# Delta stage: keys of a chunk transposed once and scaled for both scan directions, with the second direction's scaled keys kept in DRAM until its visit

## Chip, cores and metric

The kernel runs on one core of a Trainium2 chip. The metric is the device time of one execution in microseconds (us). The engines are TensorE (PE, whose weight loads are listed as PEld), VectorE (DVE), ScalarE (ACT), GpSimd (POOL) and SyncE (SP), which issues most of the transfers. [...]

## What is computed

The program is one layer of a hybrid backbone over 128 context tokens and 2048 latent tokens. The part that matters here is a gated delta rule, run once forward and once backward over the tokens, with four heads of 128 by 128 state each:

```python
def gated_delta_chunked(q, k, v, g, beta, s0):
    """S_t = a_t (I - b_t k_t k_t^T) S_{t-1} + b_t k_t v_t^T, o_t = S_t^T q_t."""
    ...
    def step(s, inp):
        q_i, k_i, u_i, w_i, g_i, qk_i = inp
        v_new = u_i - jnp.einsum("bhck,bhkv->bhcv", w_i, s)
        o_i = (jnp.einsum("bhck,bhkv->bhcv", q_i * jnp.exp(g_i)[..., None], s)
               + jnp.einsum("bhcs,bhsv->bhcv", qk_i, v_new))
        g_last = g_i[..., -1:]
        s = (s * jnp.exp(g_last)[..., None]
             + jnp.einsum("bhck,bhcv->bhkv", k_i * jnp.exp(g_last - g_i)[..., None], v_new))
        return s, o_i
    ...
o_fwd, s_fwd = gated_delta_chunked(q, k, v, g[:, :, 0], beta[:, :, 0], s_init[:, 0])
o_bwd, s_bwd = gated_delta_chunked(q[:, ::-1], k[:, ::-1], v[:, ::-1], ...)
o = o_fwd + o_bwd[:, ::-1]
```

The state update needs the keys of a chunk, scaled by `exp(g_last - g_i)`, with tokens on partitions. That scale differs between the directions; the keys do not.

## The kernel before

The delta stage takes about 785 to 1095 us of the span. It handles the context chunk `CTX` and 16 latent chunks of 128 tokens in 17 iterations t = 0 to 16. Iteration 0 visits `CTX` in both directions, and iteration t visits chunk t-1 in the forward direction (d = 0) and chunk 16-t in the backward direction (d = 1). So each latent chunk is visited twice: for the first time in t = 1 to 8 and for the second time in t = 9 to 16. The last visit of a direction updates no state.

One visit is the generator `chain(d, c)`. It loads the values `tv`, transposes the keys `kt` on PE into the PSUM tile `pkt` (L906, four 128 by 128 transposes) and scales them by `kd` into `ks` on ACT (L909, four instructions). After that come `p1` from the state `S` (L917), `rh` on DVE (L923), `p2` (L927) and `on` (L934), `p3` from X and rh (L938), its copy `y` on ACT (L940), `p5` from ks and y (L945) and the new state `Sn` on DVE (L951), and `p4` (L957) with its sum on DVE (L961). The state is the chain from one iteration to the next. The first two steps of a visit in iteration t+1 (values, transposes, scaling) are written in iteration t by `start_chain`.

Work that a visit needs is prepared ahead. `prepare` (two iterations ahead) loads keys and a decay row `d_g`, builds `dm` on DVE (L819) and ACT (L820), makes `na` (L832), the product `pq` on PE (L840) for a chunk's first visit, and `pt` on DVE (L846). `combine` (one iteration ahead) loads the inverted 32 by 32 blocks `xc` from the DRAM tensor `d_x` (L853), spreads them on POOL into `X` (L855) and completes the 128 by 128 inverse with small matmuls (L868, L874, L877, L888, L892) and ACT copies. The blocks are inverted by `invert` on POOL for several chunks at once; the inversions started in t = 2, 4 and 8 (called inversion 2, 3 and 4 here) lie inside this stage. An inversion loads `W` from DRAM (L141, eight transfers), works on POOL, copies one part on ACT (`xo`, L159) and stores 16 pieces to `d_x` (L166).

The PSUM pool `pre` has two buffers, which `pkt` and `pq` share. `ks` has four SBUF buffers. The order of the instructions on each engine is fixed when the program is built, by a scheduler that follows its own estimate of times; every engine then runs its list in order, and a transfer that waits on SP holds back all later ones on SP.

Of the kernel before, what the change touches and what calls it, by code (L numbers as in the profile page):

```python
# [7 lines left out]
F32 = mybir.dt.float32  # L8
F32R = mybir.dt.float32r
BF16 = mybir.dt.bfloat16  # L10
AF = mybir.ActivationFunctionType
# [3 lines left out]
P = 128  # L15
# [4 lines left out]
NT = NTOK // P  # L20
CTX = NT - 1
H = 4
# [25 lines left out]
def hybrid_step_kernel(ctx, tc, x, wmod, pv, rows, win, wab, wout, wup, wdown, s0, cst,  # L48
                       y_prompt, y_sample, state, dbg=None):
    nc = tc.nc  # L50
# [4 lines left out]
    dr = ctx.enter_context(tc.tile_pool(name="dr", bufs=1, space=DRAM))  # L55

    d_kq = dr.tile([NT, P, 2, H, P], F32, name="d_kq")
    d_v = dr.tile([NT, P, H, P], F32, name="d_v")
    d_z = dr.tile([NT, P, H, P], F32, name="d_z")
    d_uc = dr.tile([NT, P, 4, P], F32, name="d_uc")  # L60
    d_mix = dr.tile([NT, P, 8, P], F32, name="d_mix")
# [46 lines left out]
    kd = cd.tile([P, 2, NT, H], F32, name="kd")  # L108
# [8 lines left out]
    def chunk(d, t):  # L117
        return CTX if t == 0 else t - 1 if d == 0 else 16 - t
# [647 lines left out]
            f(*args)  # L766


    RB = dict(kt=8, dm=7, ka=7, na=6, qt=5, pt=4, X=7, xc=2, ys=6, y2=2, tv=6, ks=4, rh=2, y=2, on=6)
    sW = ExitStack()  # L770
    with ExitStack() as s2:
        kap = s2.enter_context(tc.tile_pool(name="kap", bufs=2, reuse_waits="tile"))
# [6 lines left out]
        ck = s2.enter_context(tc.tile_pool(name="ck", bufs=2, reuse_waits="tile"))  # L779
# [18 lines left out]
        def fetch(key, make, src):  # L798
            if key in kept:
                return kept[key]  # L800
            t = make()
            nc.sync.dma_start(t[:], src)
            if key[0] in KEEP:
                kept[key] = t
            return t
# [4 lines left out]
        def prepare(d, c):  # L810
            kt = fetch((c, 0), lambda: kqp.tile([P, H, P], F32, name="kt", tag="kt", bufs=RB["kt"]), d_kq[c, :, 0])
            dm = kqp.tile([P, H, P], F32, name="dm", tag="dm", bufs=RB["dm"])
            t = [chunk(d, i) for i in range(NT)].index(c)
# [9 lines left out]
            else:  # L823
                ka, new = kap.tile([P, 2, 512], F32, name="ka", tag="ka", bufs=RB["ka"]), c not in raw
                if new:
# [3 lines left out]
                else:  # L829
                    nc.sync.dma_start(ka[:], d_a[:, :, c])  # L830
            na = kqb.tile([P, H, P], F32, name="na", tag="na", bufs=RB["na"])
            nc.vector.tensor_tensor(f(na[:]), ka[:, 0], f(dm[:]), ALU.mult)  # L832
            res = [na, None, kt, None]
            yield res
            qt = fetch((c, 1), lambda: pk.tile([P, H, P], F32, name="qt", tag="qt", bufs=RB["qt"]), d_kq[c, :, 1])
            pq = ka[:, 1]
            if new:
# [4 lines left out]
                if c not in KEEP:  # L842
                    pq = pqt[:]
                    nc.sync.dma_start(d_a[:, 1, c], ka[:, 1])
            pt = pk.tile([P, H, P], F32, name="pt", tag="pt", bufs=RB["pt"])
            nc.vector.tensor_tensor(f(pt[:]), pq, f(dm[:]), ALU.mult)  # L846
# [48 lines left out]

        st = {}

        def chain(d, c):
            kq = prep[d, c]
            tv = fetch((c, 2), lambda: kqc.tile([P, H, P], F32, name="tv", tag="tv", bufs=RB["tv"]), d_v[c])  # L900
            yield
            final = c == chunk(d, NT - 1)
            if not final:
                pk_ = pre.tile([P, H, P], F32, name="pkt", tag="pre")
                for h in range(H):
                    nc.tensor.transpose(pk_[:, h], kq[2][:, h], ident[:])  # L906
                ks = ck.tile([P, H, P], F32, name="ks", tag="ks", bufs=RB["ks"])
                for h in range(H):
                    nc.scalar.activation(ks[:, h], pk_[:, h], AF.Copy, scale=kd[:, d, c, h:h + 1])  # L909
            yield  # L910
            S = st[d]
            X = mats[d, c]
            pt = prep[d, c][1]
# [5 lines left out]
            rh = tv  # L919
            if S is not None:  # L920
                rh = ck.tile([P, H, P], F32, name="rh", tag="rh", bufs=RB["rh"])
# [7 lines left out]
            on = (fp if first else lp).tile([P, H, P], F32, name="on", tag="on", bufs=16 if first else RB["on"])  # L929
# [9 lines left out]
            y = ck.tile([P, H, P], F32, name="y", tag="y", bufs=RB["y"])  # L939
# [58 lines left out]
        def start_chain(t):  # L998
            if t > 16:
                return []  # L1000
            gens = [chain(d, c) for d, c in items(t)]
            for g in gens:
                next(g)
                next(g)
            return gens
# [210 lines left out]
    if True:  # L1216
# [187 lines left out]
        c = order3[-1]  # L1404
# [216 lines left out]
```

## Time and profile before

| | |
|---|---|
| Time, median of 3 runs | 2793.93 us (2784.18 to 2797.48) |
| Profiled execution | 2791.89 us; its span 2790.1 us |
| Mean granted clock of TensorE | 0.972 |
| PE busy, whole span | 2654.8 us (95%) |
| DVE, ACT, POOL busy | 1907.2, 1153.1, 789.9 us (68%, 41%, 28%) |
| DMA moved | 526.79 MB, mean 189 GB/s |

The profile is of one execution. Its engine times are in us from the start of the span. A busy share over the whole span mixes stages; the delta stage is a ninth of it, and there DVE, ACT, POOL and SP take turns with PE in holding the next step back.

### The profile page before, as it was taken

The page shows a single profiled execution, that of the slowest core. Times are in us where ns is not written, and L with a number is a line of the kernel's source. Part 1 is how long each engine was busy: PE and PEld are TensorE (multiplying, and loading weights), DVE is VectorE, ACT ScalarE, POOL GpSimd, SP SyncE. Part 2 cuts the span into 40 slices and gives each one's busy share as a digit, 9 for nine tenths or more (in the row PEclk, how much of TensorE's full clock was granted, in tenths as well). Part 3 has the DMA queues.
Part 4 walks back from the last instruction along what each step waited for, and adds up shares of the span by engine and source line. Part 5 has one row for each costly group of instructions (what it writes and reads, how often), then busy time and mean ns, then how long its engine had stood idle before and what let it go on. Part 6 is the DMA issues. An engine that isn't in the chain of part 4 may idle for free.

```text
span 2790.1 us, 41624 instructions
## 1 busy us (share of the span) xinstructions
PE 2654.8 (95%) x15309; PEld 2237.8 (80%) x15309; DVE 1907.2 (68%) x2840; ACT 1153.1 (41%) x2421; POOL 789.9 (28%) x851
## 2 busy tenths in 40 slices
PE   7999999979888998999899999999999999999998
PEld 4888888767778887888788888888888878888887
DVE  3898999885657785444687777887888873225343
ACT  5423132355656666666544444432222232224221
POOL 2211011166335683222666666500000000000000
PEclk9999999989969999999999999999999999999999
DMA  7024531576597565665777777888777754236453
GB/s 275 20 72 119 151 109 43 104 190 134 154 279 195 141 227 207 219 231 184 256 278 266 265 271 262 279 263 255 235 232 222 230 184 134 94 104 211 165 173 119
DMA packets 426712, 526.79 MB, mean 189 GB/s; under 512 B 144790, under 2 KB 301964, under 8 KB 426252
## 3 DMA queue, kind: packets, MB, share of 16 engines
q1 hardware_dynamic: 406380, 506.30, 57.5%
q10 hardware_dynamic: 20128, 17.83, 1.9%
q8 instruction: 121, 1.98, 0.3%
q14 instruction: 83, 0.68, 0.1%
HBM read 342.13 MB, written 181.90 MB: 188 GB/s over the span
## 4 chain that ended last, share of the span: by engine, by line
PE 61%; DMA 5%; DVE 4%; ACT 3%; SPq 3%; POOL 2%; issue 2%; ACTq 0%; DVEq 0%; POOLq 0%
PE ps L1318 10%; PE ps L1320 10%; PE ps L1319 10%; PE ps L1147 7%; PE ps L1486 6%; PE ps L1484 6%; PE ps L1485 6%; PE psc L1232 2%; SPq L166 1%; DVE dm L819 1%; PE p L938 1%; PE p L945 1%; DMA dm<-d_g 1%; DMA d_mix<-bigB 1%; PE p L957 1%
## 5 line engine op out<-in xcount | busy, mean ns | idle before, releaser
L1377 DVE SCALAR_TENSOR_TENSOR pa<-gb,pvf,pa 128x512 f32<-128x512 f32 (+1 forms) x704 | 491.0, 733 | 65.3 <-ACT pa L1375 62.5
L1318 PE MATMUL ps<-T,wr 128*128 128x512 f32 x1232 | 480.5, 391 | 0.1
L1319 PE MATMUL ps<-T,wr 128*128 128x512 f32 x1232 | 479.9, 389 | 0.0
L1320 PE MATMUL ps<-T,wr 128*128 128x512 f32 x1232 | 479.0, 390 | 0.6 <-POOL wr L1246 0.6
L361 PE MATMUL ps<-hH,wr 128*128 128x512 f32 (+1 forms) x960 | 349.7, 369 | 6.6 <-ACT bigA L412 3.8
L362 PE MATMUL ps<-hL,wr 128*128 128x512 f32 (+1 forms) x960 | 352.4, 367 | 0.0
L363 PE MATMUL ps<-hH,wr 128*128 128x512 f32 (+1 forms) x960 | 350.6, 366 | 0.0
L1484 PE MATMUL ps<-wd,yr 128*128 128x512 f32 x748 | 292.5, 391 | 6.1 <-ACT yr L1480 5.5
L1486 PE MATMUL ps<-wd,yr 128*128 128x512 f32 x748 | 292.1, 391 | 0.4 <-DVE yr L1481 0.4
L1485 PE MATMUL ps<-wd,yr 128*128 128x512 f32 x748 | 292.1, 391 | 0.0
L1318 PEld LDWEIGHTS ps<-T,wr 128*128 128x128 f32 x1232 | 231.4, 188 | 49.2 <-issue 0.8
L1320 PEld LDWEIGHTS ps<-T,wr 128*128 128x128 f32 x1232 | 231.4, 188 | 49.1 <-POOL wr L1246 1.1
L1319 PEld LDWEIGHTS ps<-T,wr 128*128 128x128 f32 x1232 | 231.4, 188 | 47.4
L375 DVE SCALAR_TENSOR_TENSOR acc<-bigA,pvt,acc 128x1024 f32<-128x1024 f32 (+2 forms) x168 | 252.3, 1502 | 13.2 <-ACT acc L372 9.2
L361 PEld LDWEIGHTS ps<-hH,wr 128*128 128x128 f32 x960 | 184.0, 193 | 33.5 <-ACT bigA L412 4.2
L1481 DVE TENSOR_TENSOR yr<-yt,yr 128x1408 fp32r<-128x1408 f32 x68 | 110.5, 1625 | 143.4 <-ACT yr L1480 143.3
L363 PEld LDWEIGHTS ps<-hH,wr 128*128 128x128 f32 x960 | 185.4, 193 | 25.4 <-issue 3.0
L362 PEld LDWEIGHTS ps<-hL,wr 128*128 128x128 f32 x960 | 185.3, 193 | 24.0 <-issue 1.6
L1351 POOL TENSOR_TENSOR up<-up,x 128x512 f32<-128x512 f32 x44 | 57.3, 1302 | 413.2 <-ACT pa L1383 217.9
L375 DVE SCALAR_TENSOR_TENSOR acc<-bigC,pvt,acc 128x1024 f32<-128x1024 f32 (+2 forms) x108 | 156.6, 1461 | 24.9 <-DMA bigB<-d_uc 15.5
L1484 PEld LDWEIGHTS ps<-wd,yr 128*128 128x128 f32 x748 | 141.0, 188 | 36.6 <-ACT yr L1480 6.5
L1486 PEld LDWEIGHTS ps<-wd,yr 128*128 128x128 f32 x748 | 141.0, 188 | 30.7 <-DVE yr L1481 1.4
(360 smaller groups left out, 4571.2 us busy)
## 6 DMA issues: line engine op xcount, KB each, us to landing
d_w<-wr SPq DMA_DIRECT2D x154, 512.0 KB
wr<-d_w SPq DMA_DIRECT2D x154, 512.0 KB
yt<-d_y SPq DMA_DIRECT2D x68, 704.0 KB
raw<-in_wup_dram SPq DMA_DIRECT2D x60, 512.0 KB
xt<-in_x_dram SPq DMA_DIRECT2D x34, 512.0 KB
wmt<-in_wmod_dram SPq DMA_DIRECT2D x24, 512.0 KB
wt<-in_win_dram SPq DMA_DIRECT2D x24, 512.0 KB
wmt<-in_wmod_dram SPq DMA_DIRECT2D x48, 256.0 KB
```

What stands on the lines that cost most here:

```text
L361: nc.tensor.matmul(ps[:, 0:n], wr[:, 0, k], hH[bi][:, k], start=(k == 0), stop=False)
L362: nc.tensor.matmul(ps[:, 0:n], wr[:, 0, k], hL[bi][:, k], start=False, stop=False)
L363: nc.tensor.matmul(ps[:, 0:n], wr[:, 1, k], hH[bi][:, k], start=False, stop=(k == KD - 1))
L375: nc.vector.scalar_tensor_tensor(dst, src[:, o + t:o + t + n], w[:, t:t + 1], dst, ALU.mult, ALU.add)
L1147: nc.tensor.matmul(pss[hf][:], a[:, k], w[k][:, 512 * hf:512 * hf + 512], start=(w is woH and a is mH and k == KD - 1), stop=(w is woL and ...
L1318: nc.tensor.matmul(ps[:], h, T[i][:, 0, k], start=(first and k == 0), stop=False, skip_group_check=True)
L1319: nc.tensor.matmul(ps[:], h, T[i][:, 1, k], start=False, stop=False, skip_group_check=True)
L1320: nc.tensor.matmul(ps[:], l, T[i][:, 0, k], start=False, stop=(k == HK - 1), skip_group_check=True)
L1377: nc.vector.scalar_tensor_tensor(rows(a), src, w[:, t:t + 1], rows(a), ALU.mult, ALU.add)
L1484: nc.tensor.matmul(ps[:], yr[:, 0, i], wd[:, 0], start=(q == 0 and i == 0), stop=False)
L1485: nc.tensor.matmul(ps[:], yr[:, 0, i], wd[:, 1], start=False, stop=False)
L1486: nc.tensor.matmul(ps[:], yr[:, 1, i], wd[:, 0], start=False, stop=(q == 1 and i == HN - 1))
```

## The change

At a chunk's first visit the keys are transposed once and scaled for both directions. The scaled keys of the direction that is not being visited go into a tile with a single buffer (tag `ks2`), from there to the new DRAM tensor `d_ks`, and are loaded into a `ks` buffer at the chunk's second visit. `CTX` is visited by both directions at once and keeps both tiles in SBUF. The `ks` tag has three buffers in place of four. Lines 59 to 895 of before become one line higher in the changed kernel, and those behind the new code 20 lines higher (L906 becomes L914, L909 L922, L166 L167, L853 L854, L945 L965).

```diff
+    d_ks = dr.tile([NT, P, H, P], F32, name="d_ks")
...
-    RB = dict(kt=8, dm=7, ka=7, na=6, qt=5, pt=4, X=7, xc=2, ys=6, y2=2, tv=6, ks=4, rh=2, y=2, on=6)
+    RB = dict(kt=8, dm=7, ka=7, na=6, qt=5, pt=4, X=7, xc=2, ys=6, y2=2, tv=6, ks=3, rh=2, y=2, on=6)
...
+        other = {}
+
         def chain(d, c):
             kq = prep[d, c]
             tv = fetch((c, 2), lambda: kqc.tile([P, H, P], F32, name="tv", tag="tv", bufs=RB["tv"]), d_v[c])
             yield
             final = c == chunk(d, NT - 1)
-            if not final:
+            if c in other:
+                ks = other[c]
+                if ks is None and not final:
+                    ks = ck.tile([P, H, P], F32, name="ks", tag="ks", bufs=RB["ks"])
+                    nc.sync.dma_start(ks[:], d_ks[c])
+            else:
                 pk_ = pre.tile([P, H, P], F32, name="pkt", tag="pre")
                 for h in range(H):
                     nc.tensor.transpose(pk_[:, h], kq[2][:, h], ident[:])
-                ks = ck.tile([P, H, P], F32, name="ks", tag="ks", bufs=RB["ks"])
-                for h in range(H):
-                    nc.scalar.activation(ks[:, h], pk_[:, h], AF.Copy, scale=kd[:, d, c, h:h + 1])
+                ks, ks2 = None, None
+                for e in (d, 1 - d):
+                    if c == chunk(e, NT - 1):
+                        continue
+                    far = e != d and c != CTX
+                    kx = ck.tile([P, H, P], F32, name="ks", tag="ks2" if far else "ks", bufs=1 if far else RB["ks"])
+                    for h in range(H):
+                        nc.scalar.activation(kx[:, h], pk_[:, h], AF.Copy, scale=kd[:, e, c, h:h + 1])
+                    if e == d:
+                        ks = kx
+                    elif far:
+                        nc.sync.dma_start(d_ks[c], kx[:])
+                    else:
+                        ks2 = kx
+                other[c] = ks2
             yield
```

The order of the instructions changes with it. Two places follow, inversion 2 (on ACT and PE) and inversion 4 (on SP and PE); the numbers at the names are those of buffers and matter only for telling visits apart.

ACT, around the copy `xo` of inversion 2 (iteration 3 to 4), before:

```order
455 L940 COPY y<-p_7355 128x512
456 L940 COPY y<-p_7362 128x512
457 L820 ACTIVATE dm<-dm 128x512
458 L909 ACTIVATE ks<-pkt,kd 128x128 x4
459 L841 COPY ka<-pq 128x512
460 L889 COPY y_7371<-pm_7370 64x256
461 L889 COPY y_7379<-pm_7378 64x256
462 L159 COPY xo_6293<-W_6290 128x1024
```

and in the changed kernel:

```order
457 L960 COPY y<-p_7375 128x512
458 L922 ACTIVATE ks<-pkt,kd 128x128 x4
459 L960 COPY y<-p_7382 128x512
460 L890 COPY y_7391<-pm_7390 64x256
461 L890 COPY y_7399<-pm_7398 64x256
462 L842 COPY ka<-pq 128x512
463 L922 ACTIVATE ks<-pkt,kd 128x128 x8
464 L821 ACTIVATE dm<-dm 128x512
465 L894 COPY X<-pm_7390 64x4x64
466 L894 COPY X<-pm_7398 64x4x64
467 L160 COPY xo_6294<-W_6291 128x1024
468 L922 ACTIVATE ks<-pkt,kd 128x128 x8
```

Eight scalings more stand ahead of `xo`; four of the eight in row 463 write the single `ks2` buffer, whose last content, written by row 458, is then still to be stored.

PE, in the iteration that follows (p1 of t = 5, and the product `pq` that needs the keys and queries loaded behind inversion 2), before:

```order
3218 L892 MATMUL pm_7644<-X,y_7645 64x64 x4
3219 L957 MATMUL p_7691<-y,pt 128x128 x2
3220 L840 MATMUL pq<-qt,kt 128x128 x4
3221 L917 MATMUL p_7781<-Sn,kt 128x128 x4
3222 L917 MATMUL p_7786<-Sn,kt 128x128 x4
```

and in the changed kernel:

```order
3219 L977 MATMUL p_7723<-y,pt 128x128 x2
3220 L841 MATMUL pq<-qt,kt 128x128 x4
3221 L937 MATMUL p_7825<-Sn,kt 128x128 x4
3222 L937 MATMUL p_7830<-Sn,kt 128x128 x4
3223 L869 MATMUL pm<-X,na 32x32 x4
3224 L841 MATMUL pq<-qt,kt 128x128 x4
3225 L869 MATMUL pm<-X,na 32x32 x12
```

The product in row 3220 of before is the one that uses the queries loaded last; in the changed kernel that one is row 3224, behind both p1.

SP, around the 16 stores of inversion 4 (written in t = 8 to 13), before:

```order
449 L967 DMA d_o<-on 128x512
450 L802 DMA tv<-d_v 128x512
451 L802 DMA qt<-d_kq 128x512
452 L802 DMA tv<-d_v 128x512
453 L166 DMA d_x_81<-W_6290 8x32x32 x3
454 L166 DMA d_x_81<-xo_6293 8x32x32 x4
```

and in the changed kernel:

```order
473 L803 DMA qt<-d_kq 128x512
474 L803 DMA tv<-d_v 128x512
475 L803 DMA qt<-d_kq 128x512
476 L803 DMA tv<-d_v 128x512
477 L910 DMA ks<-d_ks 128x512
478 L167 DMA d_x_82<-W_6291 8x32x32 x2
479 L167 DMA d_x_82<-xo_6294 8x32x32 x3
```

Row 477 loads the keys of the backward visit of t = 14. It stands ahead of the stores, and it takes one of three `ks` buffers, so it waits for the p5 of t = 13 in the forward direction (`p_9939`) that reads that buffer.

On PE the combine of t = 15 (`pm<-X,na`) moves too. Before, its first part stands between the two p2 of t = 14:

```order
3441 L917 MATMUL p_10056<-Sn,kt 128x128 x4
3442 L927 MATMUL p_10090<-Sn,qt 128x128 x2
3443 L868 MATMUL pm<-X,na 32x32 x8
3444 L927 MATMUL p_10090<-Sn,qt 128x128
3445 L868 MATMUL pm<-X,na 32x32 x8
```

and in the changed kernel it stands behind p1 of t = 15, with the whole of it ahead of p3 of t = 15 (`p_10349`):

```order
3432 L937 MATMUL p_10260<-Sn,kt 128x128 x4
3433 L869 MATMUL pm<-X,na 32x32 x8
3434 L947 MATMUL p_10294<-Sn,qt 128x128 x2
3435 L869 MATMUL pm<-X,na 32x32 x8
3436 L947 MATMUL p_10294<-Sn,qt 128x128 x2
3437 L947 MATMUL p_10309<-Sn,qt 128x128 x4
3438 L875 MATMUL pm<-X,ys 32x32 x8
3439 L878 MATMUL pm<-ys,X 32x32 x4
3440 L875 MATMUL pm<-X,ys 32x32 x8
3441 L878 MATMUL pm<-ys,X 32x32 x4
3442 L889 MATMUL pm_10144<-X,na 64x64 x4
3443 L889 MATMUL pm_10152<-X,na 64x64 x4
```

No transpose of keys is left in these iterations.

## Rows read from the trace of the kernel before

**Rows 1.** Busy time of the engines in stretches of 20 us of the delta stage (us from the span's start; the second column is the stretch's length, the number behind a busy time the count of instructions), then the granted clock of TensorE, the busy share of the DMA engines and GB/s; the last row is the sum over 14 stretches from 810 to 1090.

```profile
core 0: us, PE busy (x) PEld busy (x) DVE busy (x) ACT busy (x) POOL busy (x), PEclk, DMA share, GB/s
...
830.00:850.00 20.00, 18.47 (x182) 16.99 (x182) 19.82 (x46) 12.31 (x36) 14.63 (x23) 1.00 0.75 234
...
870.00:890.00 20.00, 19.75 (x284) 18.70 (x283) 11.74 (x30) 16.35 (x51) 9.12 (x23) 1.00 0.69 169
890.00:910.00 20.00, 16.23 (x187) 15.37 (x187) 9.78 (x25) 8.52 (x29) 7.99 (x21) 0.91 0.88 227
910.00:930.00 20.00, 18.88 (x264) 17.91 (x260) 19.07 (x39) 12.78 (x41) 17.59 (x26) 1.00 0.82 256
...
950.00:970.00 20.00, 19.87 (x265) 18.46 (x259) 11.49 (x34) 17.70 (x55) 6.23 (x19) 1.00 0.45 57
...
990.00:1010.00 20.00, 18.10 (x227) 16.94 (x225) 19.47 (x39) 11.81 (x38) 17.35 (x20) 0.91 0.62 215
...
1030.00:1050.00 20.00, 19.60 (x283) 18.02 (x279) 10.76 (x28) 16.25 (x50) 12.80 (x28) 1.00 0.41 113
...
sum 280.00, PE 261.31 PEld 244.15 DVE 192.28 ACT 176.38 POOL 166.81; mean PE 18.66 PEld 17.44 DVE 13.73 ACT 12.60 POOL 11.92
```

**Rows 2.** Groups of instructions by line from 785 to 1095 us: the count stands behind the x, then busy us and mean ns of one, then the idle time of the engine ahead of them and what ended it.

```profile
L909 ACT ACTIVATE ks<-pkt,kd 128x128 f32<-128x128 f32 x128 | 36.0, 384 | 1.7 <-PE pkt L906 1.0 <-PE p L945 0.6
...
L951 DVE SCALAR_TENSOR_TENSOR Sn<-Sn,egl,p 128x128 f32<-128x128 f32 x112 | 30.5, 340 | 34.5 <-PE p L945 34.5
...
L906 PE MATMUL pkt<-ident,kt 128*128 128x128 f32 x128 | 20.8, 285 | 3.0 <-DVE pt L846 3.0
```

**Rows 3.** The chain of work that ended last, around t = 8 and 9: start in us, length in us, what.

```profile
947.90 0.87 PE pkt L906 x8
950.35 0.64 PE p L938 x4
950.99 0.89 PE p L945 x8
951.88 1.08 PE pkt L906 x8
```

**Rows 4.** The same chain around inversion 2 (SPq is a transfer being issued on SP; a DMA row runs from issue to landing).

```profile
877.25 0.64 ACT dm L820
877.89 1.03 ACT ks L909 x4
880.18 1.92 ACT xo L159
883.01 0.67 SPq L166
...
888.58 2.97 DMA d_x<-W
...
894.56 1.58 SPq L141
898.35 3.24 DMA qt<-d_kq
901.73 1.36 PE pq L840 x8
903.09 3.18 PE p L917 x16
906.27 0.82 PE pm L868 x32
907.09 1.98 PE p L927 x16
```

**Rows 5.** The p5 of t = 13 (both directions): count, shortest, median and longest duration in ns, first and last start in us.

```profile
L945 PE MATMUL p<-y,ks x16: 275/275/377, 1050.8 to 1052.6; 128*128 128x128 f32 x16
```

**Rows 6.** The chain that ended last from inversion 4 to p3 of t = 15.

```profile
1040.79 2.07 ACT xo L159
...
1043.59 0.66 SPq L166
...
1050.19 0.83 SPq L166
...
1051.81 1.41 SPq L967
...
1053.74 4.56 DMA xc<-d_x
...
1058.44 1.05 POOL X L855
...
1059.53 0.59 PE pm L868 x16
...
1061.12 1.31 PE p L927 x10
1062.43 0.89 PE p L938 x8
...
1064.45 1.09 PE p L938 x8
1065.54 0.89 PE p L945 x8
...
1067.32 1.09 PE p L945 x8
1068.41 1.34 PE p L957 x12
1069.75 0.89 PE pm L892 x16
...
1073.30 0.82 PE pm L868 x32
...
1075.88 0.67 PE p L938 x6
...
1077.68 1.31 PE p L938 x10
```

## The prediction, made before the changed kernel was run

> **What bounds the kernel now.** I read the busy times by stretch first, then the groups of instructions by line, then the chain of work that ended last at two places. The stretches [rows 1] show that the delta stage has no single bound. PE is busy 261.3 of 280 us, so 18.7 us of PE idle time is all that better overlap could give there. In 950 to 970 and 1030 to 1050 PE is full (19.87 and 19.60 of 20 us), so there an instruction taken off PE shortens the stage. In 830 to 850, 910 to 930 and 990 to 1010 DVE is as full (19.82, 19.07, 19.47), so there a transpose less on PE buys little. In 890 to 910 neither is full (PE 16.23, DVE 9.78): this is inversion 2, where the chain [rows 4] runs through ACT's copy `xo`, 16 stores, eight loads of W, and the load of `qt`, for which a `pq` on PE stands waiting. Inversion 4 has such a chain too [rows 6]: `xo`, the stores, the load of `xc`, POOL's `X`, the first combine matmuls at 1059.53.
>
> **What it removes.** There are 128 transposes of keys [rows 2], four for each of 32 visits. With 17 first visits (one of CTX, 16 chunks) 68 remain, 60 go. One alone has a mean of 285 ns, but they overlap: eight in a row take 0.87 us [rows 3], 0.109 us each. All 60 are worth at most 6.5 us. I count those of the full stretches alone: two iterations in 950 to 970 and one in 1030 to 1050, 24 x 0.109 = **-2.6 us**. The bounds are 0 and -6.5.
>
> The scalings on ACT are not removed, since each visit still needs its own: 128 before and after. They move. Fourteen far visits x 4 = 56 of them, 56 x 0.384 = 21.5 us of ACT [rows 2], go from the second half of the stage to the first, some 3 us an iteration. In the second half this shortens ACT's list. DVE waits 34.5 us in all for p5 ahead of `Sn` [rows 2], but that wait ends with PE, so a shorter ACT list frees PE's idle time at best. That idle time is 18.7 us in 14 stretches, and the second half (seven stretches) would hold about 9.3 of it if it were even. I count 0 for this and keep the 9.3 as a bound of the gain.
>
> **What it adds in the first half.** The far tile has one buffer. So the next far scaling may not begin until the store of the last one has landed, and ACT takes its list in order: `y`, `ys`, `on` and `xo` behind it wait too. A `pq` or `pkt` that wants one of the two `pre` buffers waits for the far scaling to have read it. There are 14 stores and so 13 such waits. How long a store takes is bounded by the rows: 2.97 us for `d_x` from W, 3.24 for a load of `qt` [rows 4].
>
> At inversion 2 I can follow it. Eight more scalings stand ahead of `xo` on ACT, 8 x 0.384 = 3.1 us. The store of the far tile of the row before them is issued when its scaling ends, about 879 to 880 (the scalings there run from 877.89 to 878.92), and lands 2.97 us later, at about 882.5. The far four then take 1.5 us. So `xo` starts at about 884.5 in place of 880.18, +4.3. Two `d_ks` stores among SP's transfers add about 0.6 each (the SPq rows), so `qt` is issued 5.5 us later and lands at 898.35 + 3.24 + 5.5 = 907.1. Left as it was, PE would lose 5.5 us. But the order puts both p1 (3.18 us, at 903.09) ahead of that `pq` now. Behind it four matmuls (half of 1.36) and the rest of the combine (0.6) remain: p2 starts at 907.1 + 0.7 + 0.6 = 908.4 in place of 907.09, +1.3. The products then reach DVE late, in a stretch where DVE is full (19.07 of 20), so part of the delay comes again there: one `pt` and one `dm` group, which I put at 1 to 2 us. The 12 other waits lie in iterations where ACT is idle for 2 to 11 of 20 us [rows 1]; I take 1 us in all for them. Together **+4 us**. Bounds: 0, if the idle time takes it all, and +10 (the 5.5 uncovered, and once more 2.97 + 1.5).
>
> [...] The rows give about 3 us for a store to DRAM. [...]
>
> Traffic: 14 stores and 14 loads of 0.262 MB are 7.3 MB. At the 169 to 256 GB/s of the busier stretches [rows 1] one takes 1.0 to 1.6 us of all engines, and only 890 to 910 and 910 to 930 come near full (0.88, 0.82). I count 0 beside the bounds above.
>
> **What it moves in the second half.** Each load of `ks` needs a buffer, and with three of them the backward visit's load of iteration t+1 waits for the forward p5 of t. Behind it on SP stand loads that are needed an iteration or more later, with one exception: the 16 stores of inversion 4. Their load waits for the forward p5 of t = 13, which ends at about 1051.8 (the p5 of both directions start from 1050.8 to 1052.6 [rows 5]). Before, the stores were over by 1051.0 and `xc` was issued at 1053.74 [rows 6]. They take about 0.65 us each, 10.4 in all, so now 1051.8 + 10.4 + 1.5 (two `d_o`) = 1063.7; the load takes 4.56, POOL's X 1.05, and the first combine of t = 15 can start at 1069.4 in place of 1059.53: 9.9 us late. Yet in the new order PE does nothing of that combine until behind p1 of t = 15. That p1 ran at 1071.29 with 4.5 us of combine ahead of it, and would now run at about 1066.8. So PE idles for 2.6 us, and then the whole combine runs uncovered: 11.1 us from 1059.53 to 1070.64 before, less the other work in it (1.31 + 0.89 + 1.09 + 0.89 + 1.09 + 1.34 = 6.6), is 4.5, plus some 2.5 for ACT's copies that no longer lie beside other matmuls, 7 in all. X is ready at 1076.8 and p3 of t = 15 starts then, in place of 1075.88: +0.9. Of t = 16's combine 0.82 us of matmuls and their followers ran before that p3 (1073.30), and now run behind it, +1.7 to 2. Together **+3 us**, bounds 0 (PE gets there late anyway) and +9.9 (the lateness shows whole).
>
> **The sum.** -2.6 + 4 + 3 = +4.4. Against the profiled execution's 2791.89 us that is 2796.3; the median of the three runs, 2793.93, lies 2.0 above the profiled one, so I say **2798 us**. About 0.5%, 14 us, is what a measurement of this kernel can tell from no change: faster means below 2780, slower above 2808.
>
> **Rivals.**
> - *The gain shows whole.* The waits hide in idle time and all 60 transposes count: -6.5, 2787. For it: PE is busy 93% of the stage. Against it: three stretches where DVE is full. With most of the 9.3 us of idle time on top, -15.8 and 2778 would be the end of it, which is faster; nothing shows that much released. Chance 0.20, of which 0.07 beyond 0.5%.
> - *The single far buffer decides.* Store, far scaling, `pre` buffer and the next `pkt` or `pq` form a ring that PE stands in. Each of the 13 waits can show up to 2.97 us, 38.6 us; if half shows it is +19, 2813, slower. It decides from 1.1 us a wait on (14 / 13). For it: ACT runs in order and `pre` has two buffers. Against it: where the far scaling comes, the store has often had half an iteration to land. [...] Chance 0.20.
> - *The held-up SP queue shows whole* at inversion 4: +9.9 in place of +3, 2805. For it: SP's order is fixed. Against it: PE has p1 and p2 to do meanwhile. Chance 0.10.
> - *That the change doesn't do what it says* is half true by its text: it saves transposes, not scalings, and the sum reckons with that.
>
> **How the numbers follow.** The forecast as summed has 0.50. Its own range, by the bounds of its terms, is 2790 to 2808. Faster 0.07 (from the first rival); slower 0.25 (the second's 0.20, 0.03 of the forecast's upper tail, 0.02 of the third); the rest, 0.68, is within 0.5%. The range 2780 to 2816 leaves out the first rival's far end and the upper half of the second, some 0.2.
>
> **What would show it.** In the changed profile: 68 transposes and 128 scalings; no `pkt` on PE after about 960; `xo` of inversion 2 later by 4 to 5 us and `qt`'s landing by 5 to 6, with p2 of t = 5 little later; the stores of inversion 4 starting after the forward p5 of t = 13, and p3 of t = 15 waiting for X; 950 to 970 holding more work of later iterations than before. Waits of ACT for `d_ks` of more than 15 us in all, or of PE for far scalings, would speak for the second rival; PE idle for 5 us or more at t = 15 for the third. I would be wrong above all if the many small moves in the order, which I followed at two places, add up to more than these.

## The result, and the profile after

| | before | changed |
|---|---|---|
| Median on the same chip | 2788.46 us (5 runs, 2784.18 to 2797.48) | 2814.77 us (5 runs, 2812.07 to 2817.71) |
| Ratio to the kernel before | | 1.0088 (95%: 1.0069 to 1.0106) |
| Profiled execution | 2791.89 us, span 2790.1, clock 0.972 | 2815.38 us, span 2813.6, clock 0.964 |

The change makes the kernel slower by 0.88%, some 25 us. On a second chip the same kernel gave 1.0085 (1.0055 to 1.0115).

Busy times of the changed kernel, in the columns of [rows 1]:

```profile
core 0: us, PE busy (x) PEld busy (x) DVE busy (x) ACT busy (x) POOL busy (x), PEclk, DMA share, GB/s
...
950.00:970.00 20.00, 16.27 (x197) 14.87 (x196) 13.21 (x38) 17.30 (x46) 4.41 (x15) 0.88 0.57 102
...
1070.00:1090.00 20.00, 19.32 (x227) 17.59 (x228) 0.00 (x0) 9.57 (x34) 7.05 (x10) 0.52 0.22 76
1090.00:1110.00 20.00, 19.21 (x127) 17.46 (x125) 7.00 (x20) 7.20 (x24) 3.20 (x3) 0.71 0.26 87
```

The last rows are the surprise. PE counts as busy for 19.32 of 20 us in 1070 to 1090, but its granted clock (the TensorE clock that the profile shows for a stretch, as a share of full speed) is 0.52, and DVE does nothing (0.00 us). The kernel before had this there:

```profile
1070.00:1090.00 20.00, 20.00 (x259) 19.14 (x256) 9.85 (x30) 10.45 (x35) 6.41 (x6) 1.00 0.20 71
```

The groups that answer [rows 2], for the changed kernel:

```profile
L922 ACT ACTIVATE ks<-pkt,kd 128x128 f32<-128x128 f32 x128 | 35.8, 384 | 13.5 <-DMA d_ks<-ks 12.2 <-PE pkt L914 1.1
...
L971 DVE SCALAR_TENSOR_TENSOR Sn<-Sn,egl,p 128x128 f32<-128x128 f32 x112 | 30.6, 340 | 48.0 <-PE p L965 47.9
...
L914 PE MATMUL pkt<-ident,kt 128*128 128x128 f32 x68 | 10.7, 286 | 0.6 <-ACT ks L922 0.6
```

There are 68 transposes and 128 scalings, as forecast. ACT waited 12.2 us for `d_ks` stores, in four waits, and DVE's wait for p5 grew from 34.5 to 47.9 us.

**Where the time went.** The last `Sn` of an iteration (start of its last instruction, plus its 0.34 us) cuts the stage into pieces that can be compared between kernels. The two ends of one such piece, t = 5 and t = 8, with t = 6 between them, first before and then changed:

```profile
L951 DVE SCALAR_TENSOR_TENSOR Sn<-Sn,egl,p x8: 333/334/334, 920.7 to 922.5; 128x128 f32<-128x128 f32 x8
...
L951 DVE SCALAR_TENSOR_TENSOR Sn<-Sn,egl,p x8: 333/334/334, 933.1 to 938.1; 128x128 f32<-128x128 f32 x8
...
L951 DVE SCALAR_TENSOR_TENSOR Sn<-Sn,egl,p x8: 343/343/348, 967.7 to 969.5; 128x128 f32<-128x128 f32 x8
```

```profile
L971 DVE SCALAR_TENSOR_TENSOR Sn<-Sn,egl,p x8: 343/344/344, 914.7 to 916.5; 128x128 f32<-128x128 f32 x8
...
L971 DVE SCALAR_TENSOR_TENSOR Sn<-Sn,egl,p x8: 336/340/349, 931.2 to 938.2; 128x128 f32<-128x128 f32 x8
...
L971 DVE SCALAR_TENSOR_TENSOR Sn<-Sn,egl,p x8: 339/343/348, 970.1 to 972.6; 128x128 f32<-128x128 f32 x8
```

That is 47.0 us before and 56.1 changed. Read in the same way for all pieces (us; the last is up to the first matmul behind the stage):

| kernel | t 1 to 5 | t 5 to 8 | t 8 to 13 | t 13 to 15 | t 15 to the end of the stage |
|---|---|---|---|---|---|
| before | 76.6 | 47.1 | 84.2 | 29.1 | 12.9 |
| changed | 71.2 | 56.1 | 81.3 | 42.6 | 16.4 |
| changed, second chip | 73.1 | 55.7 | 81.3 | 44.8 | 16.7 |

Of the 23.5 us between the two profiled executions, t = 1 to 5 gave back 5.4, t = 5 to 8 cost 9.0, t = 8 to 13 gave back 2.9, and t = 13 to the end of the stage cost 17.0. Some 6 us more lie outside these pieces, nearly all behind the stage.

**The waits for the stores.** The 9.0 us at t = 5 to 8 are not ACT's waits for the far store. The three long ones of the four end at these times (start, length, engine, what; in brackets the idle time ahead):

```profile
893.65 1.14 ACT L922 ACTIVATE ks<-pkt,kd 128x128 f32<-128x128 f32 x4 [3.53 <-DMA d_ks<-ks]
...
899.99 0.37 ACT L922 ACTIVATE ks<-pkt,kd 128x128 f32<-128x128 f32 x1 [3.69 <-DMA d_ks<-ks]
...
973.54 1.14 ACT L922 ACTIVATE ks<-pkt,kd 128x128 f32<-128x128 f32 x4 [3.77 <-DMA d_ks<-ks]
```

Two of them, and the short one at 875.5, lie ahead of t = 5, where the changed kernel is faster than the kernel before. The third begins at 969.8, behind the copies `y` of t = 8, so the last `Sn` of t = 8 didn't wait for it. In each case the store was issued late, behind other transfers on SP: at 889.79 behind the 16 stores of inversion 2 (the scaling that it stores had ended by 882.0), at 896.48 behind eight loads of W, at 969.82 behind the 16 stores of inversion 3. ACT went on 3.5 to 3.9 us after the issue.

**The end of the stage.** The chain of the changed kernel that answers [rows 6]:

```profile
1056.11 0.35 SPq L167
...
1066.16 3.15 DMA xc<-d_x
...
1069.37 1.05 POOL X L856
...
1070.47 0.59 PE pm L869 x16
...
1077.84 1.83 PE pm L889 x16
...
1082.09 2.00 PE p L958 x8
```

PE at the same combine (idle time ahead in brackets), two rows of before and one of the changed kernel:

```profile
1059.53 0.59 PE L868 MATMUL pm<-X,na 32*32 32x32 f32 x16 [1.58 <-POOL X L855]
...
1066.43 0.89 PE pm L888 x16
```

```profile
1070.47 0.59 PE L869 MATMUL pm<-X,na 32*32 32x32 f32 x16 [3.63 <-POOL X L856]
```

The combine of t = 15 starts at 1070.47; before, it started at 1059.53. PE waited for it already before, for 1.58 us. Sixteen L889 matmuls take 1.83 us; before, sixteen of the same line (L888) took 0.89 us. That is the halved clock: 0.50 in 1072 to 1080, and 1.00 before in 1064 to 1072. p3 of t = 15 starts at 1082.09, where my sum had 1076.8.

Why the stores start late (at 1053.8, those of `xo` at 1055.8; before at 1040.1 and 1042.9) is seen on POOL. The steps of inversion 4 (L152, L153 changed), and the copy `xo` behind them, before:

```profile
L152 POOL TENSOR_TENSOR W<-W,prod x31: 249/598/1169, 975.4 to 1039.7; 128x31 f32<-128x31 f32 x2, 128x60 f32<-128x60 f32 x2, 128x87 f32<-128x87 f32 x2, 128x112 f32<-128x112 f32 x2
...
L966 POOL TENSOR_TENSOR on<-on x7: 1278/1657/2867, 989.0 to 1040.1; 128x512 f32<-128x512 f32 x7
```

and changed, with the p5 of t = 13 as the last row:

```profile
L153 POOL TENSOR_TENSOR W<-W,prod x31: 249/626/1058, 979.5 to 1053.4; 128x31 f32<-128x31 f32 x2, 128x60 f32<-128x60 f32 x2, 128x87 f32<-128x87 f32 x2, 128x112 f32<-128x112 f32 x2
...
L986 POOL TENSOR_TENSOR on<-on x8: 1261/1576/2257, 994.3 to 1046.6; 128x512 f32<-128x512 f32 x8
L160 ACT COPY xo<-W x1: 1993/1993/1993, 1053.8 to 1053.8; 128x1024 f32<-128x1024 f32 x1
L965 PE MATMUL p<-y,ks x16: 275/275/377, 1050.9 to 1052.6; 128*128 128x128 f32 x16
```

Inversion 4 begins 4.1 us later than before and takes 73.9 us from its first step to its last, where it took 64.3. In the new order eight sums of the two directions' results (`second`, L986) stand among its steps on POOL; before there were six, the seventh row at 1040.1 being behind the last step. The eight sums take 12.5 us there, the six took 10.8; most of the other 7.9 us is POOL waiting, for the sums' `on`, for `xc` and for ACT, with the inversion queued behind. POOL's waits between the first step and the last, before (4.7 us) and changed (11.9):

```profile
POOL on L966 <- DVE on L961: 4.0, 4, 2.2
POOL X L855 <- ACT on L934: 0.7, 1, 0.7
```

```profile
POOL on L986 <- DVE on L981: 5.8, 3, 2.7
POOL X L856 <- DMA xc<-d_x: 2.5, 1, 2.5
POOL X L856 <- ACT dm L821: 1.5, 1, 1.5
POOL X L856 <- ACT X L882: 1.4, 1, 1.4
POOL on L986 <- ACT dm L821: 0.7, 1, 0.7
```

The p5 for which the `ks` load ahead of the stores waits ended by about 1052. The stores had nothing to store until POOL was through at 1053.7, and those of `xo` until 1055.8.

What counts is how far the inversion is ahead of PE. Before, its last step starts 14.4 us ahead of the last `Sn` of t = 13 (1039.7 against 1054.1), and in the changed kernel 0.8 us (1053.4 against 1054.2).

### The profile page after: what moved, and what is told of

It reads as the page before. It is cut to its first block, busy times and chain, and to the rows that moved or that the text cites. A ratio compares the mean times of both kernels' runs of the same rounds, so it can differ in the third digit from the quotient of the medians.

```text
span 2813.6 us, 41535 instructions
## 1 busy us (share of the span) xinstructions
PE 2673.7 (95%) x15249; PEld 2251.7 (80%) x15249; DVE 1903.9 (68%) x2840; ACT 1152.1 (41%) x2421; POOL 790.3 (28%) x851
## 4 chain that ended last, share of the span: by engine, by line
PE 56%; DMA 3%; DVE 2%; ACT 1%; issue 1%; POOL 1%; SPq 0%; ACTq 0%; DVEq 0%; POOLq 0%
PE ps L1338 9%; PE ps L1340 9%; PE ps L1339 9%; PE ps L1167 6%; PE ps L1506 6%; PE ps L1504 6%; PE ps L1505 6%; PE psc L1252 2%; DMA ws<-in_wdown_dram 1%; PE pt L1203 0%; DVE ps L1273 0%; DVE pa L1397 0%; POOL wr L1266 0%; DMA raw<-in_wup_dram 0%; DMA wf<-in_wout_dram 0%
## 5 line engine op out<-in xcount | busy, mean ns | idle before, releaser
L363 PEld LDWEIGHTS ps<-hL,wr 128*128 128x128 f32 x960 | 185.6, 193 | 24.2 <-issue 1.6
L376 DVE SCALAR_TENSOR_TENSOR acc<-bigC,pvt,acc 128x1024 f32<-128x1024 f32 (+2 forms) x108 | 155.1, 1447 | 25.4 <-DMA bigB<-d_uc 14.4
L1506 PEld LDWEIGHTS ps<-wd,yr 128*128 128x128 f32 x748 | 140.7, 188 | 30.9 <-DVE yr L1501 1.7
```

Source lines behind the costliest of these rows:

```text
L363: nc.tensor.matmul(ps[:, 0:n], wr[:, 0, k], hL[bi][:, k], start=False, stop=False)
L376: nc.vector.scalar_tensor_tensor(dst, src[:, o + t:o + t + n], w[:, t:t + 1], dst, ALU.mult, ALU.add)
L1506: nc.tensor.matmul(ps[:], yr[:, 1, i], wd[:, 0], start=False, stop=(q == 1 and i == HN - 1))
```

## The experiments

**Run 1: is it the wait or the clock?** The changed kernel with idle matmuls on PE ahead of the combine of t = 15 (`warm` holds its two visits); the combine is written behind p1 for it:

```diff
+            if key in warm:
+                for i in range(17 if d == 0 else 2):
+                    nc.tensor.matmul(pm[:, i % 4], st[d][:, i % 4], st[d][:, i % 4], start=True, stop=True)
             for S, E, so in pairs:
                 for h in range(H):
                     nc.tensor.matmul(pm[E, h, 0:32], na[S, h, E], X[S, h, so], start=True, stop=True)
```

> The changed kernel with 19 matmuls of 128 by 128 more on PE, whose result nothing uses (they write the combine's PSUM tile before the combine overwrites it), placed at t = 15 between p1 and the combine of t = 15, where PE waited 3.6 us for X in the changed kernel and its granted clock then fell to 0.5 until about 1100. Theory (the wait costs mostly through the clock): PE stays busy there, the clock of 1070 to 1100 is 0.9 or more, the stage ends near 1098 in place of 1110, and the time is 10 to 13 us below the changed kernel's 2814.8, some 2803. Rival (the clock is no cause; the late inverse is the whole price): the clock falls anyway or the work behind it is no shorter, and the time is the same or up to 1 us longer.

2803.66 us, 1.0062 (1.0038 to 1.0086) of before. The time is as the theory said, but its mechanism is not what happened. The clock still fell:

```profile
1064.00:1072.00 8.00, 7.12 (x96) 6.46 (x96) 0.00 (x0) 5.13 (x19) 3.94 (x6) 0.71 0.24 83
1072.00:1080.00 8.00, 7.89 (x96) 6.93 (x96) 0.00 (x0) 2.90 (x11) 0.61 (x2) 0.50 0.01 3
```

t = 13 to 15 took 43.8 us, no less than in the changed kernel. The wait filled nearly whole (0.96 us of it remained) was not enough to keep the clock through the combine that follows, whose chain runs on ACT from 1067.36 to 1070.42, ahead of the matmuls of L896. Of the 19 us by which its profiled execution is shorter than that of the changed kernel, some 10 lie ahead of t = 13 (6 of them ahead of t = 1) and 11 behind the stage, where the code is the same, while t = 13 to the end of the stage took 2 us more; its executions range from 2796 to 2817 us. I draw nothing from its lower total.

**Run 2: the other order on SP.** The load of the far result is written one step later, which puts it behind the stores:

```diff
             if c in other:
                 ks = other[c]
-                if ks is None and not final:
-                    ks = ck.tile(...)
-                    nc.sync.dma_start(ks[:], d_ks[c])
...
+            if c in other and ks is None and not final:
+                ks = ck.tile(...)
+                nc.sync.dma_start(ks[:], d_ks[c])
             if S is not None:
                 p1 = pch.tile([P, H, P], F32, name="p1", tag="ch")
```

> The changed kernel with the load of the far result written one step later in a visit (with p1), which puts the load for the backward visit of t = 14 behind the 16 stores of inversion 4 on SP; everything else of the change stays, the single far buffer too. Theory (SP's order at inversion 4 is the cause): the first store starts at 1040 to 1043 and not behind the p5 of t = 13, X of t = 15 is there by 1059 to 1060, no fall of the clock before 1090, the stage ends at 1093 to 1097, time 2797 to 2802. Rival (the ring of the single far buffer in the first half): the time stays within 4 us of 2814.8.

2801.30 us, 1.0062 (1.0040 to 1.0084). The time fits, and the predicted mechanism again does not: `xo` ran at 1046.3, since POOL's order was as bad as in the changed kernel (inversion 4 took 70.3 us), so it wasn't SP's order that had held the stores. And the load, now behind them, came too late:

```profile
PE p L965 <- DMA ks<-d_ks: 8.9, 1, 8.9
```

PE waited 8.9 us in the middle of p5 of t = 14. In this order the load waits for the stores; in the order of the changed kernel the stores did not wait for the load, as the times above show.

**Run 3: two far buffers.** The memory comes from `kt`.

```diff
-    RB = dict(kt=8, ...
+    RB = dict(kt=7, ...
-  tag="ks2" if far else "ks", bufs=1 if far else RB["ks"])
+  tag="ks2" if far else "ks", bufs=2 if far else RB["ks"])
```

> The changed kernel with two far buffers in place of one; the memory comes from the key tiles, seven buffers in place of eight. SP's order at inversion 4 stays as in the changed kernel. Theory (SP's order at inversion 4): the waits of ACT for the stores, 12.2 us in the changed profile, go, yet the time moves by no more than 4 us from 2814.8 and the clock falls at 1070 again. Rival (the single far buffer): 10 us or more below the changed kernel.

2795.71 us, 1.0036 (1.0021 to 1.0051). So the theory of the first three runs falls in part: the single buffer is a large part of the loss. ACT's waits for stores went from 12.2 us to 1.8, and t = 5 to 8 back to 47.4 (the ends of t = 5, 6 and 8):

```profile
ACT ks L922 <- DMA d_ks<-ks: 1.8, 1, 1.8
...
L971 DVE SCALAR_TENSOR_TENSOR Sn<-Sn,egl,p x8: 342/342/348, 904.7 to 906.5; 128x128 f32<-128x128 f32 x8
...
L971 DVE SCALAR_TENSOR_TENSOR Sn<-Sn,egl,p x8: 335/335/339, 924.6 to 928.1; 128x128 f32<-128x128 f32 x8
...
L971 DVE SCALAR_TENSOR_TENSOR Sn<-Sn,egl,p x8: 342/344/348, 952.1 to 953.9; 128x128 f32<-128x128 f32 x8
```

The two ways differ, though. t = 5 to 6 took 15.6 us before, 21.7 in the changed kernel and 21.6 here, so the second buffer gives nothing back there. t = 6 to 8 took 31.4, 34.4 and 25.8: the 8.6 us that it gives back lie there alone, in iterations with no wait for a store ahead of their `Sn`. That the second buffer takes this loss away is shown; that the waits for the store were the loss is not. The order of the instructions changes with the buffer too (in the changed kernel PE has a clock of 0.88 in 950 to 970, and there it waits 1.6 us for `ys` and 1.4 us for `y` from ACT), and by which path the single buffer acts stays open.

The end of the stage stayed as bad: t = 13 to 15 took 42.0 us.

**Run 4: the gain alone.** The kernel before; a second visit scales the keys as they lie in SBUF, without transposing them.

```diff
-                pk_ = pre.tile([P, H, P], F32, name="pkt", tag="pre")
-                for h in range(H):
-                    nc.tensor.transpose(pk_[:, h], kq[2][:, h], ident[:])
+                if c in seen:
+                    pk_ = kq[2]
+                else:
+                    ...
```

> The kernel before without the 60 repeated transposes and with nothing in their place: a chunk's second visit scales the keys as they are, untransposed, so the state of t above 8 is another. ACT's work is as before, and the far buffer, the store and the load do not exist. It measures the gain that there was to have. My sum said 2.6 us with 6.5 as the end: 2782 to 2788 against 2788.5 to 2794 of before. Rival (PE is not what holds these iterations): within 1 us of before. Rival (the whole effect): 6 us or more below.

2797.96 us, 1.0033 (1.0017 to 1.0049): slower than before, with 60 transposes less and nothing added. No theory had this case. The stores start here at 1041.9, 1.8 us later than before, and SP holds no load ahead of them; yet PE arrives ahead of X, waits 3.1 us, and its clock falls:

```profile
1059.25 0.87 PE L868 MATMUL pm<-X,na 32*32 32x32 f32 x16 [3.11 <-POOL X L855]
```

```profile
1070.00:1090.00 20.00, 20.00 (x173) 18.49 (x172) 2.59 (x9) 7.17 (x23) 0.61 (x2) 0.52 0.01 2
```

Here too the scheduler put the combine of t = 15 behind t = 14, as in the changed kernel, and inversion 4 took 71.7 us:

```profile
L152 POOL TENSOR_TENSOR W<-W,prod x31: 250/616/1152, 969.9 to 1041.6; 128x31 f32<-128x31 f32 x2, 128x60 f32<-128x60 f32 x2, 128x87 f32<-128x87 f32 x2, 128x112 f32<-128x112 f32 x2
```

t = 13 to 15 took 43.6 us. So the loss at the end of the stage needs neither the far buffer nor `d_ks`. It comes with a PE that is earlier, in an order made for it, and an inverse that is no earlier: its last step starts 3.7 us ahead of the last `Sn` of t = 13.

**Runs 5 to 8: take the sums off POOL.** On one chip, on which the kernel before has a median of 2783.63 us: the changed kernel again; the changed kernel and the kernel before with the sums of t = 9 to 13 on DVE; and the changed kernel without these sums.

```diff
-        def second(c, on, other):
-            nc.gpsimd.tensor_tensor(on[:], on[:], other[:], ALU.add)
+        def second(c, on, other, eng=None):
+            (eng or nc.gpsimd).tensor_tensor(on[:], on[:], other[:], ALU.add)
...
-                        second(c, ons[d, c], half[c])
+                        second(c, ons[d, c], half[c], nc.vector if t < 14 else None)
```

> The changed kernel as it is, once more, on the chip of the next three runs. All theories: 0.8 to 1.0% above the kernel before; inversion 4 takes 70 us or more from its first step on POOL to the copy xo (74.6 in the changed profile, 65.1 before), and the granted clock is near 0.5 for 20 us or more behind 1055.

> The changed kernel with the sums of the two directions' results for t = 9 to 13 on DVE in place of POOL; all else of the change stays (far buffer, store, load, three ks buffers). New theory (inversion 4 on POOL is what ends last, since the new order puts eight sums between its steps and POOL waits for them; PE then idles, its clock falls, and the combine of t = 15 runs uncovered): inversion 4 takes 60 us or less, X of t = 15 is ready before PE wants it, the clock stays at 0.9 or more until 1085, and the time is 17 to 28 us below the changed kernel of the run before. Rival (the far buffer and the d_ks transfers cost it): 5 us below at most. Rival (DVE is full in 990 to 1030 and loses what POOL gains): 5 to 12 us below.

> The kernel before with the same sums on DVE, and nothing of the change. If inversion 4's chain already set the end of the stage before (PE waited 1.6 us for X there, and 26.9 us of POOL's idle time lies ahead of the sums), 2 to 8 us below the kernel before; if PE and DVE set it, within 2 us, or above it by the 7 us of DVE work that is added.

> The changed kernel without the sums for t = 9 to 13: the second direction's result is stored alone, so the first direction's share is missing from those chunks. It takes the sums off POOL without putting them on DVE. New theory: as with the sums on DVE or up to 6 us faster, 17 to 32 us below the changed kernel. Rival (the far buffer and the transfers): 5 us below at most.

| | median, us | ratio to before (95%) | t 5 to 8 | t 8 to 13 | t 13 to 15 |
|---|---|---|---|---|---|
| changed | 2810.63 | 1.0085 (1.0055 to 1.0115) | 55.7 | 81.3 | 44.8 |
| changed, sums on DVE | 2795.56 | 1.0041 (1.0023 to 1.0059) | 55.7 | 87.9 | 32.2 |
| changed, without the sums | 2791.86 | 1.0022 (1.0004 to 1.0040) | 55.7 | 81.0 | 30.9 |
| before, sums on DVE | 2780.74 | 0.9986 (0.9969 to 1.0003) | 45.2 | 87.3 | 27.0 |

With the sums on DVE, inversion 4 takes 65.3 us in the changed kernel, the combine of t = 15 stands between the matmuls of t = 14 again, and 1070 to 1090 has its clock:

```profile
L153 POOL TENSOR_TENSOR W<-W,prod x31: 248/627/1218, 973.4 to 1038.7; 128x31 f32<-128x31 f32 x2, 128x60 f32<-128x60 f32 x2, 128x87 f32<-128x87 f32 x2, 128x112 f32<-128x112 f32 x2
...
1070.00:1090.00 20.00, 20.00 (x258) 19.11 (x259) 11.56 (x34) 8.27 (x28) 5.69 (x6) 1.00 0.13 41
```

By the medians the sums on DVE give 15 us of the 27, and leaving them out 19 (by the ratios 12 and 18 of 24). The profiles put the difference of the two in t = 8 to 13, where the sums take DVE's time. 60 us or less for inversion 4 was too much to expect (65.3). t = 5 to 8 keeps its 55.7 us, so the other part of the loss is there still. Not the length of inversion 4 decides but its lead on PE: in all 14 profiles of this case, where its last step starts more than 13 us ahead of the last `Sn` of t = 13, t = 13 to 15 takes 27 to 32 us, and where it is 4 us or less, 38 to 45. With the lead the order changes as well, as above, and no run separates the two. For the kernel before the same edit gives nothing that its interval settles.

**Runs 9 to 11: both causes at once, and what is left of the gain.** Run 9 joins the edits of runs 3 and 6; run 10 joins those of runs 4 and 7; run 11 is run 7 again.

> The changed kernel with two far buffers (seven key buffers in place of eight) and with the sums of t = 9 to 13 on DVE: both suspected causes taken away at once. If the loss is these two (9 us at t = 5 to 8 from the single far buffer, 15 to 17 us from inversion 4's chain), 8 to 12 us below the run that had only the sums on DVE (2795.6), 2783 to 2788, and not below the kernel before with the same sums on DVE by more than 3 us. If the store and load themselves cost, or the three ks buffers, it stays at 2792 or more.

> The kernel before without the 60 repeated transposes (a second visit scales untransposed keys, so its states are others), with nothing in their place, and with the sums of t = 9 to 13 on DVE. It shows what the transposes are worth once inversion 4 does not decide. By 0.109 us each at most 6.5 us below the kernel before with the sums on DVE (2780.7); my sum said 2.6. If PE is not the bound in these iterations, within 1.5 us of it.

> The kernel before with the sums of t = 9 to 13 on DVE, once more and in more rounds, beside the two runs ahead of it. By the run of it before, 0.14% below the kernel before with 0.31% on either side at most; if that was a gain, the interval now lies below 1.

| | median, us | ratio to before (95%) | t 1 to 5 | t 5 to 8 | t 8 to 13 | t 13 to 15 |
|---|---|---|---|---|---|---|
| 9: changed, two far buffers, sums on DVE | 2782.44 | 0.9991 (0.9979 to 1.0004) | 68.3 | 47.6 | 93.7 | 26.9 |
| 10: before, no second transposes, sums on DVE | 2788.81 | 1.0014 (0.9996 to 1.0032) | 71.7 | 45.0 | 82.5 | 28.1 |
| 11: before, sums on DVE | 2785.67 | 0.9992 (0.9977 to 1.0008) | 76.7 | 47.1 | 85.5 | 27.1 |

Run 9 brings the whole loss back, as expected: with two buffers and POOL free of the sums, the changed kernel is where the kernel before is. In sum with what the change gains, the store, the load and three `ks` buffers cost nothing that can be measured. They may still cost something: run 9 gains 8.4 us up to t = 5 on run 11, and loses 8.2 in t = 8 to 13, where both have the sums on DVE. There PE waits in the middle of p5 of t = 9 for a `y`, and ACT ahead of that `y` for the load of a `d_g` (the second row is of the line that makes `dm` from it):

```profile
976.60 2.08 PE L965 MATMUL p<-y,ks 128*128 128x128 f32 x8 [7.93 <-ACT y L960]
```

```profile
973.33 1.28 ACT L821 ACT_TABLE_LOAD   x1 [6.64 <-DMA dm<-d_g]
```

On SP a `d_ks` store, the eight loads of W and three loads of `ks` stand ahead of that load; what each of them costs was not separated. Run 10 shows the end of what there was to have: without the second transposes the time is not lower than run 11 to within some 0.2%. (Its profiled execution, 2779.66 us, is one of its fastest; its median says otherwise.) None of these beats the kernel before beyond its interval.

**Run 12: the clock once more.** Run 1 with 23 in place of 19 idle matmuls ahead of and between the first combine matmuls, and 24 more that the scheduler put into the gaps of the rest of that combine:

```diff
+                    pw = pre.tile([P, 512], F32, name="pw", tag="pre")
+                    for i in range(24):
+                        nc.tensor.matmul(pw[:, (i % 4) * P:(i % 4 + 1) * P], st[1][:, i % 4], st[1][:, i % 4], start=True, stop=True)
```

> The changed kernel with matmuls whose result nothing uses on PE at t = 15: 23 ahead of and between the first combine matmuls, as in the first run, and 24 more in the gaps of the rest of that combine. They add up to 5 us of their own behind the wait for X. Theory (PE's thin work, the wait and the combine alone, is what the clock falls on): the granted clock stays at 0.9 or more from 1060 to 1085, the time from the first combine matmul of t = 15 to the end of the stage falls from 40 us to 30 or less. Rival (the clock falls there for another reason): it is near 0.5 again, and this time grows by some 5 to 10 us.

2804.75 us, 1.0064 (1.0043 to 1.0086). Now the clock stays:

```profile
1064.00:1072.00 8.00, 8.00 (x84) 7.79 (x82) 6.00 (x18) 0.00 (x0) 1.04 (x1) 1.00 0.56 154
1072.00:1080.00 8.00, 8.00 (x122) 7.60 (x120) 0.00 (x0) 2.83 (x11) 6.09 (x7) 1.00 0.45 162
```

and in the changed kernel the same stretches had:

```profile
1064.00:1072.00 8.00, 4.37 (x46) 4.05 (x44) 5.03 (x15) 0.51 (x2) 2.63 (x3) 0.94 0.70 208
1072.00:1080.00 8.00, 7.79 (x98) 7.23 (x98) 0.00 (x0) 4.81 (x18) 4.45 (x6) 0.50 0.28 102
```

From POOL's X of t = 15 to the last `Sn` of t = 15 it takes 22.9 us (1070.4 to 1093.3) in place of 27.4 (1069.4 to 1096.8), although some 30 idle matmuls lie in it, 6.5 us in all (an estimate: two records each, as the 8 matmuls of p5 have 16 [rows 5], of the 0.109 us that a transpose takes [rows 3]). So the halved clock is worth about 4.5 + 6.5 = 11 us there, an estimate from these rows. What work that does something would save in those gaps was not tried. From the first combine matmul to the start of the stage's last sum it takes 33.7 us (1071.5 to 1105.2) in place of 40.1 (1070.5 to 1110.6), not the 30 that I wrote.

## Why the prediction was off, step by step

- **Transposes, -2.6.** Counts and the 0.109 us were right. That they shorten the stage was wrong: run 4 is slower without them and run 10 no faster. A row that shows PE full in 20 us says that PE worked there, not that the next step waited for nothing else. The sign that I had named for it, more work of later iterations in 950 to 970, came out the other way (PE 16.27 us at a clock of 0.88, before 19.87 at 1.00). Inversion 4's chain ended last at the combine of t = 15 already before (PE waited 1.58 us for its X), and a faster PE only arrives there sooner.
- **First half, +4.** The size was near (t = 1 to 8: 127.3 against 123.7, +3.6), its working was not, so that is luck. Inversion 2, where I had put most of it, cost nothing at its own place: `xo` started at 877.8 and not 4 us behind the 880.2 of before, and t = 4 to 5 took 24.2 us against 26.4. What happened is +9.0 at t = 5 to 8 against a gain of 5.4 before it. Of the 9.0, 6.1 came at t = 5 to 6 and remain with two buffers (run 3). The waits for stores were 4 and not 13, 12.2 us in all, and they came where I had not looked: I let a store start when its scaling ends, but it stands in SP's list behind an inversion's transfers. The rival of the single far buffer was right that the buffer decides a large part (run 3 against the changed kernel: 14 us by the ratios, 8.7 us in t = 5 to 8 by the profiles, where I had 19), but the ring of waits that it describes isn't shown: three of the four waits lie where the kernel did not get slower. A store held its buffer for 3.5 to 3.9 us from its issue, where I had 2.97 from another store.
- **Inversion 4, +3.** This is the step that failed. X's lateness was right to 1 us (1070.47 against 1069.4), by luck, since it came from another cause: not SP's load in front of the stores, whose p5 was done by about 1052, but POOL, which finished at 1053.7. I had looked at POOL's busy time and not at what its order puts between the inversion's steps. And the price was 17 and not 3, mostly because I let PE run the uncovered combine at full clock (the clock alone is about 11 us, the estimate of run 12). The working also adds up wrong by a little: 1069.4 + 7 is 1076.4 and not 1076.8. The rival of the held-up queue, at +9.9, had the same two faults.
- **The clock.** [Rows 1] show 0.91 in 890 to 910, with 3.8 us of PE idle in it (20 - 16.23), ahead of the `pq` that waited for `qt`. I read the wait there and left the clock out. In the same trace, PE waits 3.77 us for that `qt` and starts at 901.73, and the clock is 0.62 in 902 to 904, 0.53 in 904 to 906 and 1.00 from 906 to 910. In the changed kernel it is 0.94 in 1064 to 1072, where PE waits 3.63 us for X, then 0.50 in 1072 to 1080 and 0.52 in 1070 to 1090. Run 1 adds that with this wait nearly filled the clock fell all the same in the thin work behind it (short matmuls with gaps between them: PE busy for 3.43 of 4 us in 1070 to 1074, at 0.50).
- **Sum and range.** The effect forecast was +4.4 us and was +25; the time, 2814.77, lies just inside the upper end of 2816, which the far buffer's rival had set. The forecast's own range, 2790 to 2808, does not hold it. That the wider one does is luck: it was widened for the cost of one rival, and two causes filled it.

**Still open.** About 3 to 6 us of the changed profiles lie behind the stage, where the code is the same; single executions of one kernel differ by 10 to 20 us (29 of the kernel before on one chip: 2776.88 to 2795.23 us, at mean clocks of 0.978 to 0.969), and no run separates this. Why the scheduler's order puts two more sums among the inversion's steps was not followed into its estimate of times. Each run's edit is ordered anew by the scheduler, so no run separates the work that was moved or left out from the order that came with it. That the clock falls on thin work rests on one pair of runs (1 and 12: 0.50 and 1.00 in 1072 to 1080), which differ in the wait ahead of that work too (0.96 us and 0.2); where between them it would hold was not tried.

## What to carry to other kernels

Before pricing work that is taken off the fullest engine, find the next chain that ends at the same place, and see how much room it has: here PE already waited 1.6 us for a POOL inversion, so the gain turned into a wait. When a scheduler orders by its own estimate, read what the new order puts between the steps of each long serial chain, on the quiet engines too: here eight sums stood among inversion 4's steps on POOL in place of six, and POOL's waits there grew from 4.7 us to 11.9. A wait on PE is priced with the clock behind it (here 3.63 us of wait, then a clock of 0.50, worth about 11 us by the estimate of run 12). Where a buffer is stored before it is reused, count the time for which the store stands in its queue too: here the write had ended by 882.0, the store was issued at 889.79 behind 16 others, and ACT went on at 893.65. A second buffer is cheap to try. And see in which iteration a wait lies before a loss is put down to it.

## What the runs showed of the hardware

- The late combine of t = 15 (32 by 32 and 64 by 64 matmuls, with p2 among them) ran in the changed kernel with PE listed as busy for 7.79 of 8 us in 1072 to 1080, yet at a granted clock of 0.50. So the busy share did not tell of the clock here. With 128 by 128 matmuls ahead of it and in its gaps (run 12) the clock stayed at 1.00 from 1064 to 1096.
- After run 2's wait of 8.9 us the clock was back in the next stretch under dense work: 0.76 in 1050 to 1070 with PE busy for 11.1 us, and 0.99 in 1070 to 1090. In the changed kernel a wait of 3.63 us, with thin work behind it, was followed by 0.52 in 1070 to 1090. So what came behind the wait mattered more here than its length.

```profile
1050.00:1070.00 20.00, 11.11 (x85) 10.49 (x84) 6.08 (x19) 3.75 (x12) 7.15 (x7) 0.76 0.50 126
1070.00:1090.00 20.00, 19.49 (x290) 17.99 (x289) 8.34 (x22) 9.88 (x35) 5.21 (x7) 0.99 0.08 28
```
